# Forget gates by softplus with their scans moved forward, and the adaLN rows of the first FFN respread, in a two-layer diffusion trunk

## The chip, the cores and the metric

The kernel runs on one core of one Trainium2 chip. The metric is the device time of one execution in microseconds (us), taken as the median of several runs of the same program. Beside it stands one profiled execution, whose trace gives every time in this text that is shorter than the whole: PE is the matmul engine (TensorE), DVE is VectorE, ACT is ScalarE, POOL is GpSimd, SP is the engine from whose queue all weight transfers are issued.

## The reference

The trunk has two layers over 256 latent tokens and 256 context tokens of width 1024. A layer modulates its input (adaLN), runs four branches over it (a bidirectional mLSTM, differential attention, a 2-D Fourier mix, a spatial gating unit), merges them with sigmoid gates and a projection, and then runs a gated convolutional FFN. Two pieces matter here.

The modulation of a layer is a product of a conditioning vector with a large matrix; the six parts of 1024 are the shifts, scales and gates of the layer:

```python
mod  = (silu(c)     @ w_ada[l] + b_ada[l]).reshape(B, 6, 1, D)
modc = (silu(c_ctx) @ w_ada[l] + b_ada[l]).reshape(6, 1, D)
h = rmsnorm(x, norm_g[l, 0]) * (1.0 + mod[:, 1]) + mod[:, 0]
...
x = x + mod[:, 5] * rmsnorm(conv_ffn(h, ...), norm_g[l, 3])
```

The mLSTM takes per head, direction and token an input gate `ic` and a forget gate `fc`, the latter as a log sigmoid. Its decay weights come from running sums and running maxima over the tokens:

```python
fc = log_sigmoid(gg[:, 1])               # = -softplus(-gg)
b = cumsum(fc)
m_t = maximum(b + m, max over s of (b_t - b_s + ic_s))
wt = exp(b_t - b_s + ic_s - m_t)
```

## The kernel before, in words

All large products run on PE with each fp32 operand split into two fp32r parts, `hi` and `lo`, and three matmuls per product (`mm3`, L134 to L137). A weight tile is loaded by SP into a buffer `raw` (four of them), ACT writes `hi` from it (L122), and DVE or POOL writes `lo = raw - hi` (L131). PSUM results of these products use three buffers, so PE can't start a tile until the tile three before it has been read.

The program is written in one order; a scheduler with its own cost estimates then fixes the order of each engine's queue, by priority (the order of writing, shifted by `later(n)`) and by when it believes an instruction can start. At run time each engine takes its queue strictly in that order, SP's queue of transfers too. `issue_after(ins)` queues instructions on the engine of `ins` behind it.

**Gates.** In `mlstm()` the 16 gate columns `Gt` are turned by PE into `pg` (L983) and ACT adds the bias, `G` = mlG (L986). Input gates lie on partitions 0 to 3 (forward) and 32 to 35 (backward), forget gates on 64 to 67 and 96 to 99. L990 to L993 form the log sigmoid: DVE takes -|g| (mlE), ACT applies Exp and then Ln, DVE subtracts that from min(g, 0) (mlL). L1012 and L1013 copy the two groups of four rows down to partitions 0 and 32. Then come four scans of 256 tokens for the running sum `Bt` = mlB (L1007, two directions by two halves), `U = Bt - G` (L1016), four scans for the running minimum `NM` = mlNM (L1007), `EM = exp(NM - Bt)` = mlEM (L1019, L1020). PE turns U and EM into `pu` (L1027). The projections of q and k (`qk_tiles`: PE tiles qk, ACT L941 and L950, DVE L945, L947 and L951) are written after the gates but their matmuls run meanwhile; after `pu` PE goes on with the projection of the output gates (tile mm). `Bt` and `NM` are first set to zero by POOL (L928, L929). The tiles of this stage can be opened only when those of the spatial gating unit before it are done with.

**adaLN rows.** 128 outputs of the modulation are one row: a 512 KB transfer into a buffer `ar` and one product with a sum along the row on DVE (L232, `scalar_tensor_tensor` with an accumulator) for each conditioning vector. A row for latent and context tokens takes two such instructions (a junk and an ar one), a row for latent tokens alone one. `tick(n)` takes the next n rows of the list `todo`. 24 rows run in the mixer of layer 0 (one for each merged tile). In the FFN of layer 0, 56 rows run: 8 of layer 0 (part 5, the last gate), then 16 of layer 1 (its first shift and scale), all 24 with two instructions, then 32 of layer 1 with one. Three rows are taken after each up tile from the sixth on (`tu=3`), one after each down tile of the first two segments (`to=1`). The rows use two `ar` buffers, and the transfer of a row is written right before its product.

**FFN.** An up tile is 24 matmuls into `ua` and 24 into `ug` (512 columns in layer 0); ACT and DVE then form the convolution (ACT L1482, DVE L1486 and L1488), ACT the Silu (L1490), DVE the product with ug (L1491). 22 up tiles come in segments of 6, 8 and 8, each followed by the down products of the segment. Layer 1 begins with the modulation by rows 0 to 15 of its list (DVE L300).

Of the kernel before, what the change touches and what calls it, by code (L numbers as in the profile page):

```python
# [22 lines left out]
KF = 22  # L23
EPS = 1e-6
SEGS = ((0, 6), (6, 14), (14, 22))
CFG = dict(hi=4, raw=4, tb=0.6, tw=0.8, tw1=1.0, x1=2, mm=3, paddk=8, tk=4, acc=2, f3=(2, 2), qa=(0, 0), f0=(1, 1), f1=(1, 2), f2=(1, 2), n0=(1, 1), n1=(1, 1), hd=1, hq=3, na=48, tu=3, to=1, ka=2, yp=3, ph=400, kh=4, kt=4, ld=2, dl=2, W=2, h0=3, mix=1, keep=4, hot=400, nst=6, nb=1, pt=(1, 0), w1=14, w2=6, wd=(24,), ahead={7: (0, -1, 1), 0: (2,), 1: (3,)}, so=("mddddfddd", "mdpf", "mpf", "mrpfd0q"), xr="pppppppp", fw=(0, 2), g0="nddddddd", g1=("nddddddn", "nddddddn"), g3=("nddddddn", "ndndndnd"), gy="nddddddn", cm=1, h1=2, xp=2, pf=(1, 1), ck=1, ys=(1, 1, 1, 1), c0=1, te=0.8)
# [9 lines left out]
def trunk_kernel(ctx: ExitStack, tc: tile.TileContext, I, out):  # L36
    nc = tc.nc
# [39 lines left out]

    turn = [0.0, CFG["tb"]]
    todo = []
    sq = []  # L80
    hold = [None, False]
    wn = [0]
# [1 line left out]
    more_on = []  # L84
    x = {}

    def open_ada(stack, side, ns):
        pool = stack.enter_context(tc.tile_pool(name="adap", bufs=1, side=side))
        scb = pool.tile([128, ns, 1024], F32, name="scb")
        junk = pool.tile([128, 1024], mybir.dt.bfloat16, name="junk") if ns == 2 else None  # L90
        return pool, scb, junk

    def init_ada(ad):
        pool, scb, junk = ad
        ns = scb.shape[1]
        nc.sync.dma_start(out=scb, in_=I["ccb"][:, 0:ns, :])
        e = pool.tile([128, 1024], F32, name="ar", tag="ar", bufs=2)
# [56 lines left out]
    @contextmanager  # L154
    def later(n):
        p = tc.cur_priority
        tc.cur_priority = p + n
        yield
        tc.cur_priority = p + (tc.cur_priority - p - n)
# [64 lines left out]
            op=ALU.add)  # L224
        return ins_of(at)

    def ada_row(ad, i, m, ns, mod, vec):
        pool, scb, junk = ad
        raw = pool.tile([128, 1024], F32, tag="ar", name="ar", bufs=2)
        nc.sync.dma_start(out=raw, in_=I["w_adaT"][i])  # L230
        for st in range(ns):
            nc.vector.scalar_tensor_tensor(out=raw if st == ns - 1 else junk, in0=raw, scalar=0.5, in1=scb[:, st, :],  # L232
                                           op0=ALU.mult, op1=ALU.mult, accum_out=mod[:, m, st:st + 1])
        if m % 8 == 7:
            o = mod[:, m - 7:m + 1, 0:ns]
            nc.vector.tensor_tensor(
                out=o, in0=o, op=ALU.add,
                in1=vec[:, V_BA + m - 7:V_BA + m + 1].rearrange("p (a o) -> p a o", o=1).to_broadcast([128, 8, ns]))

    def mod_scale(vec, mod, chunk, gi, plus, ns=2, k0=0, k1=8, o=None):  # L240
        if o is None:
# [406 lines left out]
    def layer(l):  # L648
# [15 lines left out]
        with ExitStack() as es:  # L664
# [251 lines left out]
            def mlstm():  # L916
# [67 lines left out]
                U = w3.tile([128, T], F32, name="mlU", tag="mlU")  # L984
                G = wk.tile([128, 512], F32, tag="sq", name="mlG")
                nc.scalar.activation(out=G, in_=ps, func=AF.Identity, bias=vec[:, V_GB:V_GB + 1], scale=1.0)  # L986
                E1 = wk.tile([128, 512], F32, tag="t1", name="mlE")
                L1 = wk.tile([128, 512], F32, tag="t2", name="mlL")
                r = slice(64, 128)
                nc.vector.scalar_tensor_tensor(out=E1[r], in0=G[r], scalar=-1.0, in1=G[r], op0=ALU.mult, op1=ALU.min)  # L990
                nc.scalar.activation(out=E1[r], in_=E1[r], func=AF.Exp)
                nc.scalar.activation(out=E1[r], in_=E1[r], func=AF.Ln, bias=1.0, scale=1.0)
                nc.vector.scalar_tensor_tensor(out=L1[r], in0=G[r], scalar=0.0, in1=E1[r], op0=ALU.min, op1=ALU.subtract)  # L993

                def scans(dst, src, po, pi, d0, op0, op1, init):
                    for d in range(2):
                        o = slice(po[d], po[d] + 4)
                        i = slice(pi[d], pi[d] + 4)
                        if d == 0:
                            rng = (slice(256, 512), slice(0, 256))  # L1000
                            tail = 511
                        else:
                            rng = (slice(511, 255, -1), slice(255, None, -1))
                            tail = 256
                        for q in range(2):
                            a = d0[i].to_broadcast([4, 256]) if d0 is not None else src[i, rng[q]]
                            nc.vector.tensor_tensor_scan(out=dst[o, rng[q]], data0=a, data1=src[i, rng[q]],  # L1007
                                                         initial=init if q == 0 else dst[o, tail:tail + 1],
                                                         op0=op0, op1=op1)
# [285 lines left out]
            def sgu(early):  # L1295
# [16 lines left out]
                nc.sync.dma_start(out=sgw, in_=I["sgw"][l])  # L1312
                nc.sync.dma_start(out=sgb, in_=I["sgb"][l])
                sums = tiny.tile([128, 8], F32, tag="sums", name="sums")

                def take_sv(t2, ps):
                    for t in range(2):
                        with hot():
                            nc.scalar.activation(out=gv[:, t2 + t, :], in_=ps[:, t, :], func=AF.Gelu_apprx_tanh,
                                                 accum_out=sums[:, t2 + t:t2 + t + 1])  # L1320
# [48 lines left out]
            if not last or CFG["na"] < 40:  # L1369
                ad = open_ada(es, "left", ns)  # L1370
                init_ada(ad)
                todo.extend((lambda m=m: ada_row(ad, i0 + m, m, ns, mod, vec))
                            for m in range(CFG["na"] if last else 16, 40))
            diff(*(diff_tiles() if last else dqk))
            es3.close()
            fill(64)
# [87 lines left out]
        with ExitStack() as es:  # L1464
# [239 lines left out]
```

## Time and profile before

| | |
|---|---|
| median of 3 runs | 1406.83 us (1405.43 to 1408.57) |
| the profiled execution | 1407.98 us, of which the span of the engines' work is 1406.2 us |
| PE busy | 1336.9 us, 95% of the span |
| DVE busy | 863.8 us, 61% |
| POOL busy | 849.7 us, 60% |
| ACT busy | 621.6 us, 44% |
| mean granted PE clock | 0.983 of full speed |

A row of a timeline shows the start, the duration, the engine, the line, the instruction with its tiles (out<-in), how many were merged, and in brackets how long the engine had been idle before it and what ended that. A row of a list of waits shows who waited for whom: the time in total, how often, and the longest.

### The profile page before, as it was taken

Reading aid. Unit: us, or ns where it says so; the run is one execution under the profiler, and the core shown is the slowest. Engines: PE = TensorE matmul, PEld = TensorE weight load, DVE = VectorE, ACT = ScalarE, POOL = GpSimd, SP = SyncE. Lnnn points to the kernel's source line nnn. Section 1 sums busy time; section 2 is a strip of 40 time slices with the busy share of each in tenths; the row PEclk is TensorE's granted clock in tenths of the full one; section 3 lists DMA queues with packets and bytes.
Section 4 is the critical chain, followed back from the end, with each engine's and each line's share of the span. In section 5 each row is a group of like instructions: output and inputs, shape, how many; then the busy total and the mean of one; then the engine's idle time right before and its main releaser. Section 6 shows DMA issues by size and latency. Waiting matters only on the chain. (4 is left out here: it accounts for less than half of the span.)

```text
span 1406.2 us, 22765 instructions
## 1 busy us (share of the span) xinstructions
PE 1336.9 (95%) x8514; PEld 1195.1 (85%) x8514; DVE 863.8 (61%) x1554; ACT 621.6 (44%) x1098; POOL 849.7 (60%) x978
## 2 busy tenths in 40 slices
PE   8798999999999979999799999898999999899998
PEld 6597899888878979888688889897999998899997
DVE  4738766888777465599886553768847543532323
ACT  4435534444324445423231333466636545554443
POOL 1533234456764676567565546675556898689894
PEclk9999999999999999999899999999999999999999
DMA  9422223433443443466577443343324455355552
GB/s 347 137 77 81 69 105 106 135 120 140 160 162 107 147 151 114 138 227 211 195 253 270 155 160 106 116 135 104 108 76 135 147 164 184 123 184 200 183 181 75
DMA packets 61935, 210.55 MB, mean 150 GB/s; under 512 B 7145, under 2 KB 9729, under 8 KB 61569
## 3 DMA queue, kind: packets, MB, share of 16 engines
q1 hardware_dynamic: 61824, 209.10, 44.1%
q8 instruction: 67, 1.10, 0.3%
q14 instruction: 44, 0.35, 0.1%
HBM read 208.01 MB, written 1.06 MB: 149 GB/s over the span
## 5 line engine op out<-in xcount | busy, mean ns | idle before, releaser
L131 POOL TENSOR_TENSOR lo<-raw,hi 128x256 fp32r<-128x256 f32 x814 | 698.6, 890 | 392.2 <-ACT hi L122 373.9
L122 ACT CAST hi<-raw 128x1024 fp32r<-128x1024 f32 (+2 forms) x284 | 293.7, 1036 | 336.1 <-PE ua L136 76.6
L131 DVE TENSOR_TENSOR lo<-raw,hi 128x1024 fp32r<-128x1024 f32 (+2 forms) x79 | 122.3, 1548 | 89.6 <-ACT hi L122 89.5
L135 PE MATMUL gt<-hh,hi 128*128 128x512 f32 (+1 forms) x512 | 175.3, 342 | 1.0 <-DVE sig L782 1.0
L137 PE MATMUL gt<-hh,lo 128*128 128x512 f32 (+1 forms) x512 | 172.8, 338 | 0.6 <-POOL lo L131 0.6
L136 PE MATMUL gt<-hl,hi 128*128 128x512 f32 (+1 forms) x512 | 172.2, 336 | 0.0
L135 PE MATMUL ug<-hh,hi 128*128 128x256 f32 (+1 forms) x384 | 125.9, 328 | 10.4 <-DVE ca L1488 10.4
L232 DVE SCALAR_TENSOR_TENSOR ar<-ar,scb 128x1024 f32<-128x1024 f32 x80 | 122.4, 1534 | 15.6 <-DMA ar<-w_adaT 14.8
L136 PE MATMUL ug<-hl,hi 128*128 128x256 f32 (+1 forms) x384 | 125.5, 327 | 0.0
L135 PE MATMUL ua<-hh,hi 128*128 128x256 f32 (+1 forms) x384 | 124.3, 324 | 0.9 <-ACT hh L301 0.9
L137 PE MATMUL ug<-hh,lo 128*128 128x256 f32 (+1 forms) x384 | 125.1, 326 | 0.0
L136 PE MATMUL ua<-hl,hi 128*128 128x256 f32 (+1 forms) x384 | 124.0, 323 | 0.1
L137 PE MATMUL ua<-hh,lo 128*128 128x256 f32 (+1 forms) x384 | 123.8, 322 | 0.0
L137 PEld LDWEIGHTS gt<-hh,lo 128*128 128x128 f32 x512 | 96.6, 189 | 11.6 <-POOL lo L131 0.8
L135 PEld LDWEIGHTS gt<-hh,hi 128*128 128x128 f32 x512 | 96.7, 189 | 11.0 <-DVE sig L782 1.2
L136 PEld LDWEIGHTS gt<-hl,hi 128*128 128x128 f32 x512 | 96.8, 189 | 10.0
L135 PEld LDWEIGHTS ug<-hh,hi 128*128 128x128 f32 x384 | 74.2, 193 | 16.9 <-issue 8.5
L135 PE MATMUL o<-fh,hi 128*128 128x256 f32 (+1 forms) x240 | 81.0, 337 | 0.0
L136 PE MATMUL mm<-lo,hh 128*128 128x256 f32 x272 | 78.6, 289 | 2.4 <-DVE lo L131 2.4
L136 PE MATMUL o<-fl,hi 128*128 128x256 f32 (+1 forms) x240 | 80.5, 335 | 0.0
L137 PE MATMUL o<-fh,lo 128*128 128x256 f32 (+1 forms) x240 | 80.5, 335 | 0.0
L135 PEld LDWEIGHTS ua<-hh,hi 128*128 128x128 f32 x384 | 72.8, 190 | 7.6 <-ACT hh L301 1.1
(312 smaller groups left out, 3250.6 us busy)
## 6 DMA issues: line engine op xcount, KB each, us to landing
raw<-w_up SPq DMA_DIRECT2D x92, 512.0 KB, 4.0
ar<-w_adaT SPq DMA_DIRECT2D x80, 512.0 KB, 4.1
raw<-w_gate SPq DMA_DIRECT2D x64, 512.0 KB, 3.5
raw<-w_tm SPq DMA_DIRECT2D x24, 512.0 KB, 3.5
raw<-w_dr SPq DMA_DIRECT2D x22, 512.0 KB, 3.5
raw<-w_dn SPq DMA_DIRECT2D x20, 512.0 KB, 3.7
ada_w<-w_ada SPq DMA_DIRECT2D x16, 512.0 KB, 8.3
raw<-w_branch SPq DMA_DIRECT2D x16, 512.0 KB, 3.6
```

What stands on the lines that cost most here:

```text
L122: nc.scalar.copy(hi[:, :n], raw[:, :n])
L131: e.tensor_tensor(out=lo[:, s], in0=raw[:, s], in1=hi[:, s].bitcast(F32), op=ALU.subtract)
L135: nc.tensor.matmul(ps, a[0], b[0], start=start, stop=False)
L136: nc.tensor.matmul(ps, a[0], b[1], start=False, stop=False)
L137: return nc.tensor.matmul(ps, a[1], b[0], start=False, stop=stop)
L232: nc.vector.scalar_tensor_tensor(out=raw if st == ns - 1 else junk, in0=raw, scalar=0.5, in1=scb[:, st, :], op0=ALU.mult, op1=ALU.mult, ac ...
```

## The change

The log sigmoid is written as -softplus(-g): one ACT instruction with the Softplus table reads the forget gates on partitions 64 to 99 and writes partitions 0 to 35, and the sum is scanned with a subtraction. The backward scans run over 512 tokens in one instruction. The sums, U and the minima get a priority 200 places earlier. The Softplus table is asked for right after the last Gelu of the spatial gating unit. The adaLN rows of both places load one row ahead (the transfer of the next row is written before the product of this one); in the FFN of layer 0 they get three buffers, the 24 rows with two instructions are mixed evenly among the 32 with one, and up tiles take two and three rows in turn.

```diff
-CFG = dict(..., tu=3, ...)
+CFG = dict(..., tu=2.5, ..., gs=200)
...
+    due = [0.0]
-    def open_ada(stack, side, ns):
+    def open_ada(stack, side, ns, bufs=2):
...
     def tick(n=1, after=None):
         for _ in range(n):
             if todo:
-                if after is None:
-                    todo.pop(0)()
-                else:
-                    with tc.issue_after(after):
-                        todo.pop(0)()
+                row = todo.pop(0)
+                row.load()
+                for ahead in todo[:row.bufs // 2]:
+                    ahead.load()
+                with tc.issue_after(after) if after is not None else ExitStack():
+                    row.run()
...
-    def ada_row(ad, i, m, ns, mod, vec):
-        pool, scb, junk = ad
-        raw = pool.tile([128, 1024], F32, tag="ar", name="ar", bufs=2)
-        nc.sync.dma_start(out=raw, in_=I["w_adaT"][i])
...
+    class AdaRow:
...
+        def load(self):
+            if self.raw is None:
+                self.raw = self.pool.tile([128, 1024], F32, tag="ar", name="ar", bufs=self.bufs)
+                nc.sync.dma_start(out=self.raw, in_=I["w_adaT"][self.i])
+
+        def run(self):      # the products and the bias as before
...
-                E1 = wk.tile([128, 512], F32, tag="t1", name="mlE")
-                L1 = wk.tile([128, 512], F32, tag="t2", name="mlL")
-                r = slice(64, 128)
-                nc.vector.scalar_tensor_tensor(out=E1[r], in0=G[r], scalar=-1.0, in1=G[r], op0=ALU.mult, op1=ALU.min)
-                nc.scalar.activation(out=E1[r], in_=E1[r], func=AF.Exp)
-                nc.scalar.activation(out=E1[r], in_=E1[r], func=AF.Ln, bias=1.0, scale=1.0)
-                nc.vector.scalar_tensor_tensor(out=L1[r], in0=G[r], scalar=0.0, in1=E1[r], op0=ALU.min, op1=ALU.subtract)
...
-                        if d == 0:
-                            rng = (slice(256, 512), slice(0, 256))
-                            tail = 511
-                        else:
-                            rng = (slice(511, 255, -1), slice(255, None, -1))
-                            tail = 256
-                        for q in range(2):
+                        rng = (slice(256, 512), slice(0, 256)) if d == 0 else (slice(511, None, -1),)
+                        for q in range(2 - d):
...
-                nc.vector.tensor_copy(L2[0:4], L1[64:68])
-                nc.vector.tensor_copy(L2[32:36], L1[96:100])
-                scans(Bt, L2, (0, 32), (0, 32), onec, ALU.mult, ALU.add, 0.0)
+                nc.scalar.activation(out=L2[0:36], in_=G[64:100], func=AF.Softplus, scale=-1.0)
                 q = slice(0, 36)
-                nc.vector.tensor_tensor(out=U[q], in0=Bt[q], in1=G[q], op=ALU.subtract)
-                scans(NM, U, (0, 32), (0, 32), None, ALU.min, ALU.min, 0.0)
+                with later(-CFG["gs"]):
+                    scans(Bt, L2, (0, 32), (0, 32), onec, ALU.mult, ALU.subtract, 0.0)
+                    nc.vector.tensor_tensor(out=U[q], in0=Bt[q], in1=G[q], op=ALU.subtract)
+                    scans(NM, U, (0, 32), (0, 32), None, ALU.min, ALU.min, 0.0)
...
                 tm_proj(5, NTQ, take_sv)
+                table(AF.Softplus, gelu[0])
...
-                ad = open_ada(es, "left", ns)
-                todo.extend((lambda m=m: ada_row(ad, i0 + m, m, ns, mod, vec)) for m in range(40, 48))
+                ad = open_ada(es, "left", ns, 3)
+                todo.extend(AdaRow(ad, i0 + m, m, ns, mod, vec) for m in range(40, 48))
             if l == 0:
-                todo.extend((lambda m=m: ada_row(ad, 32 + m, m, 2 if m < 16 else 1, mods[1], P[1]["vec"]))
-                            for m in range(CFG["na"]))
+                nxt = [AdaRow(ad, 32 + m, m, 2 if m < 16 else 1, mods[1], P[1]["vec"]) for m in range(CFG["na"])]
+                two, lone = todo + nxt[:16], nxt[16:]
+                todo.clear()
+                for j, row in enumerate(lone):
+                    while two and len(two) * len(lone) > (len(lone) - j - 1) * 24:
+                        todo.append(two.pop(0))
+                    todo.append(row)
...
                     if i > CFG["tk"]:
-                        tick(1 if last else CFG["tu"], at[0])
+                        due[0] += 1 if last else CFG["tu"]
+                        n = int(due[0])
+                        due[0] -= n
+                        tick(n, at[0])
```

## Rows read from the trace of the kernel before

**Rows 1.** The waits of PE over the whole span: total, times, longest.
```profile
PE ug L135 <- DVE ca L1488: 10.4, 3, 7.7
```
**Rows 2.** Timeline of PE, gates of layer 1.
```profile
967.56 0.43 PE L1027 MATMUL pu<-cst,mlU 36*128 36x36 f32 x4
974.68 0.64 PE L1027 MATMUL pu<-cst,mlEM 36*128 36x36 f32 x4 [6.69 <-ACT mlEM L1020]
```
**Rows 3.** Timeline of PE, gates of layer 0.
```profile
123.61 0.44 PE L1027 MATMUL pu<-cst,mlEM 36*128 36x36 f32 x4 [1.45 <-ACT mlEM L1020]
...
128.18 0.39 PE L136 MATMUL mm<-lo,hh 128*128 128x256 f32 x1 [2.39 <-DVE lo L131]
```
**Rows 4.** Stretches after these waits: length, busy time by engine, granted PE clock, DMA share, GB/s.
```profile
128.00:134.00 6.00, 5.82 (x36) 5.82 (x37) 5.15 (x8) 1.95 (x3) 1.86 (x2) 0.72 0.48 170
975.00:980.00 5.00, 5.00 (x28) 4.93 (x28) 4.88 (x11) 3.69 (x6) 0.00 (x0) 0.58 0.17 69
680.00:689.00 9.00, 8.30 (x26) 6.72 (x27) 8.17 (x12) 3.28 (x5) 1.55 (x1) 0.69 0.53 180
```
**Rows 5.** Timeline of DVE, FFN of layer 0.
```profile
676.86 1.22 DVE L232 SCALAR_TENSOR_TENSOR junk<-ar,scb 128x1024 bf16<-128x1024 f32 x1 [3.86 <-DMA ar<-w_adaT]
...
679.81 0.74 DVE L1488 SCALAR_TENSOR_TENSOR ca<-ua,vec,ca 128x510 f32<-128x510 f32 x1
...
681.31 0.69 DVE L1491 TENSOR_TENSOR ca<-ca,ug 128x512 f32<-128x512 f32 x1 [0.76 <-ACT ca L1490]
```
**Rows 6.** DVE by line, 600 to 700 us: count, busy, mean ns, idle before.
```profile
L232 DVE SCALAR_TENSOR_TENSOR ar<-ar,scb 128x1024 f32<-128x1024 f32 x23 | 35.1, 1528 | 0.4
L232 DVE SCALAR_TENSOR_TENSOR junk<-ar,scb 128x1024 bf16<-128x1024 f32 x22 | 30.2, 1374 | 7.8 <-DMA ar<-w_adaT 7.8
L131 DVE TENSOR_TENSOR lo<-raw,hi 128x1024 fp32r<-128x1024 f32 (+1 forms) x7 | 12.0, 1712 | 0.0
```
**Rows 7.** Timeline of PE: the first ua and ug of two neighbouring up tiles.
```profile
688.58 0.39 PE L135 MATMUL ua<-hh,hi 128*128 128x512 f32 x1
...
699.46 0.39 PE L135 MATMUL ua<-hh,hi 128*128 128x512 f32 x1
```
**Rows 8.** The waits of SP's queue, 590 to 830 us.
```profile
SPq L230 <- DVE ar L232: 101.6, 45, 6.2
```
**Rows 9.** Timeline of DVE: the last adaLN row, and the first modulation of layer 1.
```profile
821.33 1.22 DVE L232 SCALAR_TENSOR_TENSOR ar<-ar,scb 128x1024 f32<-128x1024 f32 x1
...
901.95 0.87 DVE L300 SCALAR_TENSOR_TENSOR t<-x,ms,R 128x256 f32<-128x256 f32 x2 [3.96 <-POOL lo L131]
```
**Rows 10.** Timeline of ACT, gates of layer 1.
```profile
950.32 0.69 ACT L986 ACTIVATE mlG<-pg,vec 128x512 f32<-128x512 f32 x1
...
955.99 1.28 ACT L991 ACT_TABLE_LOAD   x1 [1.59 <-DVE mlE L990]
...
974.00 0.62 ACT L1020 ACTIVATE mlEM<-mlEM 36x512 f32<-36x512 f32 x1
```
**Rows 11.** Timeline of DVE, gates of layer 1.
```profile
962.61 1.39 DVE L1007 TENSOR_TENSOR_SCAN mlB<-one,mlL 4x256 f32<-4x256 f32 x2
...
968.09 2.38 DVE L1007 TENSOR_TENSOR_SCAN mlNM<-mlU 4x256 f32<-4x256 f32 x2
...
973.29 0.67 DVE L1019 TENSOR_TENSOR mlEM<-mlNM,mlB 36x512 f32<-36x512 f32 x1
```
**Rows 12.** Timeline of POOL, layer 1.
```profile
956.03 0.52 POOL L928 MEMSET mlB<- 128x512 f32 x1
...
965.15 3.62 POOL L131 TENSOR_TENSOR lo<-raw,hi 128x256 fp32r<-128x256 f32 x4 [5.35 <-ACT hi L122]
969.20 3.91 POOL L131 TENSOR_TENSOR lo<-raw,hi 128x256 fp32r<-128x256 f32 x4 [0.43 <-ACT hi L122]
```
**Rows 13.** Timeline of DVE, layer 0.
```profile
113.42 2.19 DVE L1007 TENSOR_TENSOR_SCAN mlB<-one,mlL 4x256 f32<-4x256 f32 x2
...
126.39 1.74 DVE L131 TENSOR_TENSOR lo<-raw,hi 128x1024 fp32r<-128x1024 f32 x1
```

More of the change, by code (lines that the diff above doesn't have):

```diff
@@ L25 @@
 SEGS = ((0, 6), (6, 14), (14, 22))
-CFG = dict(hi=4, raw=4, tb=0.6, tw=0.8, tw1=1.0, x1=2, mm=3, paddk=8, tk=4, acc=2, f3=(2, 2), qa=(0, 0), f0=(1, 1), f1=(1, 2), f2=(1, 2), n0=(1, 1), n1=(1, 1), hd=1, hq=3, na=48, tu=3, to=1, ka=2, yp=3, ph=400, kh=4, kt=4, ld=2, dl=2, W=2, h0=3, mix=1, keep=4, hot=400, nst=6, nb=1, pt=(1, 0), w1=14, w2=6, wd=(24,), ahead={7: (0, -1, 1), 0: (2,), 1: (3,)}, so=("mddddfddd", "mdpf", "mpf", "mrpfd0q"), xr="pppppppp", fw=(0, 2), g0="nddddddd", g1=("nddddddn", "nddddddn"), g3=("nddddddn", "ndndndnd"), gy="nddddddn", cm=1, h1=2, xp=2, pf=(1, 1), ck=1, ys=(1, 1, 1, 1), c0=1, te=0.8)
+CFG = dict(hi=4, raw=4, tb=0.6, tw=0.8, tw1=1.0, x1=2, mm=3, paddk=8, tk=4, acc=2, f3=(2, 2), qa=(0, 0), f0=(1, 1), f1=(1, 2), f2=(1, 2), n0=(1, 1), n1=(1, 1), hd=1, hq=3, na=48, tu=2.5, to=1, ka=2, yp=3, ph=400, kh=4, kt=4, ld=2, dl=2, W=2, h0=3, mix=1, keep=4, hot=400, nst=6, nb=1, pt=(1, 0), w1=14, w2=6, wd=(24,), ahead={7: (0, -1, 1), 0: (2,), 1: (3,)}, so=("mddddfddd", "mdpf", "mpf", "mrpfd0q"), xr="pppppppp", fw=(0, 2), g0="nddddddd", g1=("nddddddn", "nddddddn"), g3=("nddddddn", "ndndndnd"), gy="nddddddn", cm=1, h1=2, xp=2, pf=(1, 1), ck=1, ys=(1, 1, 1, 1), c0=1, te=0.8, gs=200)
 C_ID, C_MF, C_MB, C_RC, C_RS, C_SEL, C_ONE, C_END = 0, 128, 256, 384, 448, 512, 514, 515
@@ L90, in open_ada @@
         junk = pool.tile([128, 1024], mybir.dt.bfloat16, name="junk") if ns == 2 else None
-        return pool, scb, junk
+        return pool, scb, junk, bufs
     def init_ada(ad):
-        pool, scb, junk = ad
+        pool, scb, junk, bufs = ad
         ns = scb.shape[1]
         nc.sync.dma_start(out=scb, in_=I["ccb"][:, 0:ns, :])
-        e = pool.tile([128, 1024], F32, name="ar", tag="ar", bufs=2)
+        e = pool.tile([128, 1024], F32, name="ar", tag="ar", bufs=bufs)
         for st in range(ns):
@@ L225, in ada_fin, with __init__ @@
         return ins_of(at)
-    def ada_row(ad, i, m, ns, mod, vec):
-        pool, scb, junk = ad
-        raw = pool.tile([128, 1024], F32, tag="ar", name="ar", bufs=2)
-        nc.sync.dma_start(out=raw, in_=I["w_adaT"][i])
[L231 to L238, printed above, removed]
+    class AdaRow:
+        def __init__(self, ad, i, m, ns, mod, vec):
+            self.pool, self.scb, self.junk, self.bufs = ad
+            self.i, self.m, self.ns, self.mod, self.vec, self.raw = i, m, ns, mod, vec, None
+        def load(self):
[3 more added lines that the diff above has]
+        def run(self):
+            m, ns, mod, raw = self.m, self.ns, self.mod, self.raw
+            for st in range(ns):
+                nc.vector.scalar_tensor_tensor(out=raw if st == ns - 1 else self.junk, in0=raw, scalar=0.5,
+                                               in1=self.scb[:, st, :], op0=ALU.mult, op1=ALU.mult,
+                                               accum_out=mod[:, m, st:st + 1])
+            if m % 8 == 7:
+                o = mod[:, m - 7:m + 1, 0:ns]
+                b = self.vec[:, V_BA + m - 7:V_BA + m + 1].rearrange("p (a o) -> p a o", o=1).to_broadcast([128, 8, ns])
+                nc.vector.tensor_tensor(out=o, in0=o, op=ALU.add, in1=b)
     def mod_scale(vec, mod, chunk, gi, plus, ns=2, k0=0, k1=8, o=None):
@@ L998, in scans @@
                         i = slice(pi[d], pi[d] + 4)
-                        if d == 0:
-                            rng = (slice(256, 512), slice(0, 256))
-                            tail = 511
-                        else:
-                            rng = (slice(511, 255, -1), slice(255, None, -1))
-                            tail = 256
-                        for q in range(2):
-                            a = d0[i].to_broadcast([4, 256]) if d0 is not None else src[i, rng[q]]
+                        rng = (slice(256, 512), slice(0, 256)) if d == 0 else (slice(511, None, -1),)
+                        for q in range(2 - d):
+                            a = d0[i].to_broadcast([4, 256 * (d + 1)]) if d0 is not None else src[i, rng[q]]
                             nc.vector.tensor_tensor_scan(out=dst[o, rng[q]], data0=a, data1=src[i, rng[q]],
-                                                         initial=init if q == 0 else dst[o, tail:tail + 1],
+                                                         initial=init if q == 0 else dst[o, 511:512],
                                                          op0=op0, op1=op1)
                 L2 = wk.tile([128, 512], F32, tag="acc", name="mlL2", bufs=CFG["acc"])
-                nc.vector.tensor_copy(L2[0:4], L1[64:68])
-                nc.vector.tensor_copy(L2[32:36], L1[96:100])
-                scans(Bt, L2, (0, 32), (0, 32), onec, ALU.mult, ALU.add, 0.0)
+                nc.scalar.activation(out=L2[0:36], in_=G[64:100], func=AF.Softplus, scale=-1.0)
                 q = slice(0, 36)
-                nc.vector.tensor_tensor(out=U[q], in0=Bt[q], in1=G[q], op=ALU.subtract)
-                scans(NM, U, (0, 32), (0, 32), None, ALU.min, ALU.min, 0.0)
+                with later(-CFG["gs"]):
+                    scans(Bt, L2, (0, 32), (0, 32), onec, ALU.mult, ALU.subtract, 0.0)
+                    nc.vector.tensor_tensor(out=U[q], in0=Bt[q], in1=G[q], op=ALU.subtract)
+                    scans(NM, U, (0, 32), (0, 32), None, ALU.min, ALU.min, 0.0)
                 EM = wk.tile([128, 512], F32, tag="t1", name="mlEM")
@@ L1314, in sgu @@
                 sums = tiny.tile([128, 8], F32, tag="sums", name="sums")
+                gelu = [None]
                 def take_sv(t2, ps):
@@ L1318, in take_sv @@
                         with hot():
-                            nc.scalar.activation(out=gv[:, t2 + t, :], in_=ps[:, t, :], func=AF.Gelu_apprx_tanh,
-                                                 accum_out=sums[:, t2 + t:t2 + t + 1])
+                            gelu[0] = ins_of(nc.scalar.activation(
+                                out=gv[:, t2 + t, :], in_=ps[:, t, :], func=AF.Gelu_apprx_tanh,
+                                accum_out=sums[:, t2 + t:t2 + t + 1]))
                 tm_proj(5, NTQ, take_sv)
+                table(AF.Softplus, gelu[0])
                 mean = tiny.tile([128, 4], F32, tag="mean", name="mean")
@@ L1371, in layer @@
                 init_ada(ad)
-                todo.extend((lambda m=m: ada_row(ad, i0 + m, m, ns, mod, vec))
-                            for m in range(CFG["na"] if last else 16, 40))
+                todo.extend(AdaRow(ad, i0 + m, m, ns, mod, vec) for m in range(CFG["na"] if last else 16, 40))
             diff(*(diff_tiles() if last else dqk))
```

## The prediction

> **What bounds the kernel now.** I read the list of waits by engine first, then the timelines around PE's longest ones, then DVE's work by line in those places. PE is busy 1336.9 of 1406.2 us, so the kernel is bound by PE and only PE's idle time (69.3 us) and its clock can be won. The longest line in the list of PE's waits is a wait of the ug matmuls for the convolution on DVE [rows 1]. 7.7 us of its 10.4 are one stop, which DVE's timeline puts at 673 to 680.6 us, when that convolution ends [rows 5]. The gates hold three more: PE waits 6.69 us for EM in layer 1 [rows 2], and in layer 0 1.45 us for EM and 2.39 us for a lo [rows 3]. The change touches these four places, 18.2 us; PE's other waits lie at the start of the program, in the norms between the stages, and in the merges, where nothing is edited.
>
> Each of the three stops is followed by a stretch at the lower of PE's two clock levels, 1.2 instead of 2.4 GHz. The length of the stretch times what is missing from the granted clock is the time lost: 0.28 of 6 us is 1.7 us, 0.42 of 5 us is 2.1 us, 0.31 of 9 us is 2.8 us [rows 4], of which some 0.35 us fell in the wait itself, leaving 2.4. If PE does not stop, this comes back too. The most that can be won is then 7.7 + 2.4 = 10.1 us in the FFN, 6.7 + 2.1 = 8.8 us in layer 1, 3.8 + 1.7 = 5.5 us in layer 0: 24.4 us.
>
> **The adaLN rows.** DVE is full where the rows with two products lie: 45 products took 65.3 us of the 100 us before 700, 1.45 us each [rows 6]. At 680 two things met: DVE had a backlog, and the product at the head of its queue waited 3.86 us for its transfer, with the convolution behind it [rows 5]. PE, with three PSUM buffers, waited for that convolution.
>
> An up tile takes PE 10.88 us [rows 7]. On DVE it costs 0.74 + 0.74 + 0.69 = 2.2 us for ca [rows 5], the first convolution taken as long as the second, and lo: two weight tiles, 0.4 of them on DVE (the counter adds 0.6 per tile and POOL takes it at 1), so 0.8 x 1.71 = 1.4 us [rows 6]. Three rows with two products are 6 x 1.45 = 8.7 us: 12.3 us together, over the 10.88. Mixed, the 56 rows hold 80 products, 1.43 a row, so 2.5 rows are 3.6 products or 5.2 us: 8.8 us together. The fullest up tile of the new order has five products, 7.3 us, so 10.9 us: just full, and it comes once in the first pair and once at the end of the second segment, between emptier ones. The load does not vanish, it moves: the lone rows at the end had three products per up tile and get 3.6.
>
> The list now lasts longer. Rows taken: 5 in the two up tiles of the first segment, 8 in its down products, 20, 8, and 15 left, which are done at the sixth up tile of the last segment; before it was 6 + 8 + 24 + 8 and 10 left, done at the fourth. The last row moves from 821 us [rows 9] by two up tiles to some 843, less what is won. Row 53 of the list (counted from 0) is the last that layer 1 needs at its first modulation, at 902 us [rows 9]: 59 us of cover. The 8 rows of the last gate of layer 0 are at places 0 to 16, taken before the end of the fourth up tile's share of the second segment, and are needed only after the last segment's up tiles.
>
> The transfers: 80 in all, as before, each 512 KB. What changes is SP's queue. SP waited 101.6 us in 45 of the 56 loads of this stretch for a buffer `ar` [rows 8], with weight loads queued behind. With two buffers the load of row j waits for the product of row j-2; with three, written one row ahead, the load of row j+1 waits for that same product. So at the moment when row j was asked for before, row j+1 is asked for now, a whole row sooner, and DVE is no longer behind, so the wait itself shortens. A row is one or two products and their pause, 4.4 us if 2.5 of them share an up tile, against a worst delay of 3.86 us [rows 5]. I take 9.6 of the 10.1 us. If the cover failed once more at another place, it would cost again what it costs now, about 10 us. In the mixer of layer 0 the rows come one per merged tile and PE waits for none of them: nothing.
>
> **The gates, layer 1.** G is done at 951.0 us [rows 10]. Before, scans could only start at 962.6 [rows 11] because two DVE instructions, Exp, Ln and two table loads stood between. Softplus is not in this trace; its nearest row is the Exp of EM over the same 36 x 512, 0.62 us [rows 10], and at most it is Exp, Ln and their loads again, 2 x (0.62 + 1.28) = 3.8 us. Its own table load (1.28 us by the same row) stands before G, when ACT is waiting for the value projection. By either value its result is there at 951.6 to 954.8, and the scans then wait for something else: POOL zeroes Bt at 956.03, so they start at 956.6 [rows 12]. A scan over 256 tokens takes 0.70 us at best and 1.19 at worst [rows 11]. One over 512 lies between one and two of them, 0.7 and 1.4 (2.4 slow); I take 1.4, since nothing in the rows says that the second half is cheaper. Bt is then 2 x 0.7 + 1.4 = 2.8 us, U 0.67 (taken as long as the subtraction for EM of the same shape [rows 11]), NM 2.8, EM 0.67, a table load 1.28 and Exp 0.62: 956.6 + 8.8 = 965.4. With scans at 1.19, and U and EM taken as slow, it is 956.6 + 4.8 + 1.2 + 4.8 + 1.2 + 1.9 = 970.5. PE comes to `pu` at 967.56 [rows 2], so EM is 2.2 us early or 2.9 us late; before, 6.7 late. What is late next is DVE's queue: from 962.6 on its scans and the queue behind them run to 973 and beyond [rows 11], and the convolutions of q and k must read PSUM before PE's next tile mm can start. The edit takes mlE, mlL and two copies off that queue, some 2.7 us if each is taken at the 0.67 of the subtraction for EM [rows 11]. I expect about 1.6 us to stay of the 8.8 and take 7.2.
>
> The Trainium skill bears on the slow value: SBUF — State Buffer, section Who interferes with whom, says that a DVE instruction with two SBUF inputs contends with a GpSimd instruction that reads SBUF, and that the second to start blocks fully. The rows agree in kind: the sums at 962.6 took 0.70 us each while POOL stood idle, the minima at 968 1.19 us while it was making lo [rows 11, 12]. POOL's lo also surrounds the place to which the scans move, so by that rule the late end, 970.5, would be the one to expect. It is priced as the second case below.
>
> **The gates, layer 0.** The same chain had its scans at 113.42 [rows 13]; by layer 1's rows G precedes the scans there by 12 us [rows 10, 11]. Moved up by 6 us, as in layer 1, EM is ready well before PE's `pu` at 122.2, by both values of a scan. The 2.39 us wait is a lo that DVE began at 126.39 [rows 13], behind the scans and convolutions; it has to come 3.9 us sooner to be hidden (2.39 + 1.45). The same 2.7 us of DVE work disappear and the scans fill idle time that DVE spent waiting for Exp and Ln. I take 4.8 of 5.5.
>
> **Sum.** 9.6 + 7.2 + 4.8 = 21.6 us. The profiled execution took 1407.98, so 1386.4; it lies 1.15 above the median of the runs, which gives 1385.2. New small waits somewhere in a schedule that is laid out anew: about 1 us. **1386 us.**
>
> **Rivals.**
> - *Layer 1 keeps its wait.* DVE's queue, not the gate chain, is the limit there, the scans run at their slow rows, and PE stops for 3 us plus its stretch at the low clock: 5 of the 8.8 stay. 1386 + 3.5 = 1389.5. For it: the scans at 1.19 us in [rows 11]. Against: the work taken off.
> - *The FFN stop moves.* Rows run on through two more up tiles and the fullest has five products; a late transfer meets a full DVE once more. 1386 + 9.6 = 1395.6.
> - *Nothing comes of it.* PE arrives earlier at waits whose end does not move (the norms between layers, weights not yet split by POOL, which is 60% busy over the span), and these take it back: 1406, within 0.2% of before. Against it: where PE was not stopped, two neighbouring up tiles follow at the bare sum of their matmuls [rows 7], so weights were there ahead of it.
> - *Slower.* SP issues in order. If the loads written ahead hold SP waiting for an `ar` buffer while the next up tile's weights stand behind them, each of the 16 up tiles from the sixth to the last but one starts late. The point from which it decides is 22 / 16 = 1.4 us per up tile; at 2 us per tile it is 1386 + 32 = 1418. For it: SP already waits 101.6 us there [rows 8]. Against: three buffers for two, and products that run on time.
>
> **Chances.** The forecast 0.58, layer 1 keeps its wait 0.20, the FFN stop moves 0.09, nothing 0.06, slower 0.07. A difference under 0.2% (2.8 us) can't be told from none here. The first three cases are faster: 0.87; same 0.06; slower 0.07. The likeliest case alone spans 1382.5 (all 24.4 won, 1406.83 - 24.4) to 1390. The range for 8 in 10 reaches up to the moved FFN stop: 1382 to 1397.
>
> **What would show it.** In the new profile: no wait of ug for ca over 1 us between 590 and 850; DVE with gaps in every up tile there, where 600 to 700 had next to none; the junk products' waits for `ar` well under the 7.8 us of [rows 6]; no Exp or Ln load in the gates, Softplus once per layer right behind G, scans of Bt at about 957 in layer 1 and 107 in layer 0; waits of `pu` for EM under 2 us; the granted clock 1.00 in the stretches of [rows 4]. The prediction is wrong if PE still stops at `pu`, if a new wait of PE for DVE or SP of more than 5 us appears, or if a table load of Tanh falls between the early Softplus load and its use.

## The result, and the profile after

The changed kernel takes 1392.18 us (median of 4 runs, 1390.05 to 1396.08) against 1406.69 us before (4 runs): ratio 0.9899, 95% interval 0.9874 to 0.9924, 14.5 us faster. The forecast was 1386, the range 1382 to 1397. The profiled execution of the changed kernel is its longest run, 1396.08 us with a span of 1394.3, so the two traces differ by 11.9 us of span. The same kernel profiled once more (change_again below) has a span of 1391.9, 14.3 less than before.

PE's waits in the list of the whole span: the 7.7 us stop of ug for ca is gone, and what is left on that line is mainly a wait of 2.4 us at 522 us, ahead of the edited rows, that was there before too (2.42 us); `pu` no longer appears; and two lines have grown, qk (0.3 before) and gt for sig (one wait of 1.0 before).

```profile
PE qk L137 <- DVE qk L957: 3.2, 1, 3.2
PE ug L137 <- DVE ca L1488: 2.7, 2, 2.4
PE gt L137 <- DVE sig L792: 2.2, 2, 1.2
```

The stretches of [rows 4] in the new kernel, and first the one with and behind its new wait in layer 1 (the granted clock is the number behind the last bracket):

```profile
950.00:960.00 10.00, 6.83 (x24) 5.32 (x23) 7.23 (x13) 6.59 (x12) 1.38 (x3) 0.83 0.15 54
128.00:134.00 6.00, 6.00 (x52) 6.00 (x51) 4.85 (x8) 2.46 (x5) 5.10 (x6) 1.00 0.29 91
680.00:689.00 9.00, 9.00 (x42) 7.44 (x41) 8.21 (x12) 2.97 (x5) 6.98 (x6) 1.00 0.85 288
```

**Where the time went.** Six instructions of PE that stand in every version cut the span into stretches. In the new trace they are:

```profile
65.15 0.67 PE L877 MATMUL f<-PQ,dft 128*128 128x258 f32 x2 [0.63 <-DVE PQ L871]
334.60 0.47 PE L1235 MATMUL ds<-st,st 128*128 128x512 f32 x1 [0.69 <-DVE st L1217]
879.11 0.58 PE L172 MATMUL st<-one,sq 128*128 128x1 f32 x4 [0.74 <-DVE sq L295]
906.26 1.08 PE L857 MATMUL f<-dft,ft 128*128 128x256 f32 x2 [2.01 <-ACT ft L832]
1013.39 0.66 PE L735 MATMUL pt<-cst,fsq 128*128 128x128 f32 x4 [0.95 <-DVE fsq L728]
1194.53 0.79 PE L503 MATMUL hT<-dg,xa 128*128 128x128 f32 x2 [4.85 <-DVE dg L497]
```

The differences of their starts, in each profiled execution (us; the names are those of the experiments below):

| | to f | f to ds: layer 0's gates | ds to st: its FFN | st to ft: norms | ft to pt: layer 1's gates | pt to hT: its merge | hT to end |
|---|---|---|---|---|---|---|---|
| before | 64.3 | 275.2 | 553.7 | 26.0 | 108.5 | 179.7 | 198.9 |
| the change | 65.2 | 269.5 | 544.5 | 27.2 | 107.1 | 181.1 | 199.8 |
| change_again | 65.1 | 269.4 | 545.1 | 25.9 | 105.6 | 181.2 | 199.7 |
| gates_only | 66.0 | 269.4 | 555.5 | 26.8 | 105.9 | 181.2 | 200.1 |
| rows_only | 64.7 | 275.3 | 545.0 | 26.4 | 108.7 | 179.7 | 199.3 |
| rows_ahead | 65.3 | 275.2 | 550.1 | 26.3 | 108.6 | 179.6 | 199.2 |
| rows_mix | 64.2 | 275.8 | 548.1 | 25.4 | 110.4 | 179.7 | 199.3 |
| rows_25 | 64.1 | 273.7 | 554.5 | 26.7 | 108.8 | 179.8 | 199.3 |
| old_log | 64.6 | 273.0 | 545.2 | 26.3 | 105.2 | 181.1 | 198.6 |
| conv_first | 64.8 | 269.5 | 544.5 | 26.0 | 102.6 | 181.3 | 199.7 |
| conv_first_2 | 64.0 | 270.0 | 544.8 | 26.0 | 102.6 | 179.7 | 198.8 |
| conv_sm | 65.3 | 270.1 | 544.9 | 25.4 | 104.2 | 180.6 | 198.6 |
| no_prefetch | 65.6 | 269.5 | 544.9 | 26.2 | 108.8 | 181.1 | 200.0 |
| scan4 | 64.9 | 270.1 | 545.2 | 26.4 | 106.3 | 179.7 | 198.7 |

Layer 0's gates give 5.7 us and the FFN 9.2, both close to the forecast. Layer 1's gates give only 1.3 (2.9 in change_again), and its merge takes 1.4 back. The profiled execution loses some 1.6 us of layer 1's stretch before the gates begin: G starts 32.7 us after ft, against 31.2 before and in change_again, and the granted clock from 905 to 912 us is 0.76, against 1.00 in change_again.

**The FFN.** DVE's groups between 600 and 700 us, against [rows 6], and SP's wait for a buffer, against [rows 8]: there are 35 products instead of 45, and the junk products wait 2.4 us for a transfer instead of 7.8. The third line, from DVE's list of waits over the same 100 us, shows that DVE is no longer behind: its product with ug now waits for PE.

```profile
L242 DVE SCALAR_TENSOR_TENSOR ar<-ar,scb 128x1024 f32<-128x1024 f32 x25 | 37.8, 1538 | 0.0
L242 DVE SCALAR_TENSOR_TENSOR junk<-ar,scb 128x1024 bf16<-128x1024 f32 x10 | 16.0, 1598 | 2.4 <-DMA ar<-w_adaT 2.4
DVE ca L1491 <- PE ug L139: 8.4, 4, 2.4
```

```profile
SPq L237 <- DVE ar L242: 78.6, 39, 6.3
```

**Layer 0's gates**, against [rows 3, 13]: the scans start at 106.82, and `pu` follows without a wait, as does the tile behind it.

```profile
106.82 2.30 DVE L1005 TENSOR_TENSOR_SCAN mlB<-one,mlL 4x256 f32<-4x256 f32 x2 [0.51 <-POOL mlB L938]
```

```profile
122.80 0.41 PE L1025 MATMUL pu<-cst,mlEM 36*128 36x36 f32 x4
```

**Layer 1's gates**, against [rows 2, 10, 11]. DVE's timeline, then PE's, then ACT's. The first row of the sums, and the first of the minima, merges a scan over 256 tokens with the one over 512 (0.68 and 1.58 us, 0.82 and 1.22 us):

```profile
945.25 2.29 DVE L1005 TENSOR_TENSOR_SCAN mlB<-one,mlL 4x256 f32<-4x256 f32 x2 [1.82 <-POOL mlB L938]
947.58 1.05 DVE L1005 TENSOR_TENSOR_SCAN mlB<-one,mlB,mlL 4x256 f32<-4x256 f32 x1
948.73 0.97 DVE L1014 TENSOR_TENSOR mlU<-mlB,mlG 36x512 f32<-36x512 f32 x1
949.63 0.47 DVE L955 SCALAR_TENSOR_TENSOR qk<-qk,vec,qk 128x255 f32<-128x255 f32 x1
950.03 2.06 DVE L1005 TENSOR_TENSOR_SCAN mlNM<-mlU 4x256 f32<-4x256 f32 x2
952.12 0.74 DVE L1005 TENSOR_TENSOR_SCAN mlNM<-mlU,mlNM 4x256 f32<-4x256 f32 x1
952.79 0.45 DVE L957 SCALAR_TENSOR_TENSOR qk<-qk,vec,qk 128x255 f32<-128x255 f32 x1
```

```profile
953.38 0.47 PE L137 MATMUL qk<-hh,hi 128*128 128x512 f32 x1 [3.17 <-DVE qk L957]
...
960.91 0.41 PE L1025 MATMUL pu<-cst,mlEM 36*128 36x36 f32 x4
```

```profile
939.71 0.63 ACT L1010 ACTIVATE mlL<-mlG 36x512 f32<-36x512 f32 x1
...
942.97 0.56 ACT L951 ACTIVATE qk<-qk,vec 128x256 f32<-128x256 f32 x1
...
953.31 1.28 ACT L960 ACT_TABLE_LOAD   x1 [9.79 <-DVE qk L957]
...
954.93 0.61 ACT L1018 ACTIVATE mlEM<-mlEM 36x512 f32<-36x512 f32 x1
```

EM is ready at 955.5, and PE comes to `pu` at 960.6 without a wait for it. Most of these 5.1 us are PE's own delay, though. The first q/k tile was ready for its convolution at 943.5 (L951 ends), while DVE stood idle for POOL's memset. The two convolution steps (L955, L957) are queued between and behind the scans, until 953.2. They read that tile's PSUM buffer, one of three, and PE's fourth q/k tile needs it: 3.17 us of wait, and then 0.17 x 10 = 1.7 us lost at the lower clock. In the kernel before, DVE's timeline has the same two steps ahead of the scans, in the time in which DVE waited for Exp and Ln:

```profile
958.53 0.48 DVE L945 SCALAR_TENSOR_TENSOR qk<-qk,vec,qk 128x255 f32<-128x255 f32 x1 [2.63 <-ACT qk L941]
...
961.20 0.48 DVE L947 SCALAR_TENSOR_TENSOR qk<-qk,vec,qk 128x255 f32<-128x255 f32 x1
```

Measured from ft, which leaves the earlier gains out, PE came to `pu` 48.4 us after it before the change and EM was ready at 55.5; in change_again EM is ready at 47.7 and PE comes at 52.8.

### The profile page after: what moved, and what is told of

It is laid out like the page before. It is cut to its first block, busy times and chain, and to the rows that moved or that the text cites. A ratio compares the mean times of both kernels' runs of the same rounds, so it can differ in the third digit from the quotient of the medians.

```text
span 1394.3 us, 22736 instructions
## 1 busy us (share of the span) xinstructions
PE 1339.0 (96%) x8514; PEld 1196.5 (86%) x8514; DVE 856.8 (61%) x1542; ACT 618.5 (44%) x1096; POOL 852.5 (61%) x978
## 5 line engine op out<-in xcount | busy, mean ns | idle before, releaser
L133 DVE TENSOR_TENSOR lo<-raw,hi 128x1024 fp32r<-128x1024 f32 (+2 forms) x79 | 114.2, 1446 | 87.0 <-ACT hi L124 87.0
L138 PEld LDWEIGHTS ua<-hl,hi 128*128 128x128 f32 x384 | 73.1, 190 | 6.8 <-DVE hl L312 0.5
```

Source lines behind the costliest of these rows:

```text
L133: e.tensor_tensor(out=lo[:, s], in0=raw[:, s], in1=hi[:, s].bitcast(F32), op=ALU.subtract)
L138: nc.tensor.matmul(ps, a[0], b[1], start=False, stop=False)
```

## The experiments

Each ratio is to the kernel before, run beside it on the same chip; in brackets stands its 95% interval.

**The halves.** gates_only makes only the edits in `mlstm()` and the Softplus table request; rows_only makes only those to `tick`, `AdaRow`, the order of the list and `tu`; change_again is the change itself.

> The gate edits alone (softplus, early scans, its table prefetch); the adaLN rows as before. By the reading of the two traces layer 0 gives 5.7 us and layer 1 only 2.9, because PE's fourth q/k tile waits some 3.2 us for the first tile's convolution behind the scans: 1406.7 - 8.6 = 1398.1 us, with that wait of qk for DVE in layer 1 and the FFN stop of 7.7 us for ca still there. By the prediction's own terms it would be 4.8 + 7.2 = 12.0: 1394.7 us, and no such wait. If the qk wait comes from the rows' new order and not from the scans, it is absent here and layer 1 gives up to 8.8: 1392.2 us.

> The adaLN edits alone; the gates as before. By the reading of the traces the FFN stop is worth 9.1 us and the 2.7 us lost between the layers is a chance of the clock: 1406.7 - 9.1 = 1397.6 us, and the waits of PE for EM in both layers stay (1.5 and 6.7 us). If the longer list of rows is what costs the 2.7 us between the layers, it is 1406.7 - 6.4 = 1400.3 us, with the granted clock of that stretch at 0.80 again. If the FFN stop moves: 1406.

> The changed kernel once more. If the 2.7 us lost between the layers (granted clock 0.80 at 875 to 900 us) are a chance of one execution, that stretch has the clock of the kernel before (about 0.95) here or is again different, with a span of 1389 to 1392 us; if the change causes them, the clock is 0.80 there again. The 3.17 us wait of qk for DVE and 1.18 us wait of gt for sig belong to the order of instructions and must show again.

Measured: gates_only 0.9951 (0.9934 to 0.9968), rows_only 0.9940 (0.9921 to 0.9959), change_again 0.9884 (0.9864 to 0.9903), median 1392.93. The halves add up: 0.49% + 0.60% = 1.09% against 1.16%. They are 6.9 and 8.5 us, nearest to the first value of each expectation (8.6 and 9.1). PE's timeline of gates_only has the FFN stop and, without any new row order, the wait of qk:

```profile
677.06 0.77 PE L135 MATMUL ug<-hh,hi 128*128 128x512 f32 x1 [8.13 <-DVE ca L1479]
...
963.17 0.47 PE L135 MATMUL qk<-hh,hi 128*128 128x512 f32 x1 [3.18 <-DVE qk L947]
```

So that wait comes from the gate edits. In rows_only it is absent and `pu` waits its 6.69 us again. The 2.7 us between the layers, of which the expectations speak, are the 1.2 us of the norms stretch (26.0 to 27.2) and the 1.6 us before G. change_again, the same kernel, has neither: they belong to one execution, and the theory that the longer list costs there falls. The 1.5 us of layer 1's merge are there in gates_only and not in rows_only; more below.

**The first convolution ahead of the scans.** In layer 1 the first q/k tile is written before the scans, and the scans are queued behind its second convolution step (`conv[0]`):

```diff
...
+                if last:
+                    qk_tiles(0, 1)
-                with later(-CFG["gs"]):
+                with later(-CFG["gs"]), after(conv[0]):
...
-                qk_tiles(CFG["qa"][l], 4)
+                qk_tiles(int(last), 4)
```

> The whole change, and in layer 1 the scans are issued after the convolution of the first q/k tile, which only needs DVE's idle time before the memset of mlB. If that convolution's place in DVE's queue causes the 3.17 us wait of the fourth q/k tile and the low clock behind it (1.75 us), both go: 1392.2 - 4.9 = 1387.3 us, and EM (ready at about 955 in the run of the change) still comes in time for pu, which PE then reaches at about 955.7. If EM is late instead, PE stops at pu for up to 3 us: 1390.5 us. If the wait is for something else on DVE (the scans' own length), it only moves: 1392 us.

> conv_first once more, beside conv_sm. If the stretch of layer 1's gates (ft to the pt of fsq, 102.6 us) belongs to the order, it shows within 0.5 us again, and the time is 2 to 3 us under the change.

Measured: 1390.13 (1389.00 to 1391.14), ratio 0.9865 (0.9843 to 0.9887), against change_again's 1392.03 to 1393.67 on the same chip; and the second time 1388.08 (1387.53 to 1389.92), 0.9857 (0.9839 to 0.9875). It is faster than the kernel before and, by 2.8 us in the median, than the change. DVE's timeline and the stretch of the wait:

```profile
941.03 0.48 DVE L957 SCALAR_TENSOR_TENSOR qk<-qk,vec,qk 128x255 f32<-128x255 f32 x1
942.21 2.29 DVE L1006 TENSOR_TENSOR_SCAN mlB<-one,mlL 4x256 f32<-4x256 f32 x2 [0.70 <-POOL mlB L938]
```

```profile
950.00:960.00 10.00, 9.75 (x74) 8.93 (x73) 9.70 (x17) 6.65 (x10) 7.03 (x8) 1.00 0.32 97
```

The convolution fits into the idle time before the memset, the scans start 37.4 us after ft as in change_again, the wait of qk is gone, and the clock is 1.00. The place of the convolution in DVE's queue is thereby shown as the cause. It gave 3.0 us of the 4.9 (105.6 to 102.6): PE, earlier now, meets waits of 0.66 us for the tile tho, 0.43 and 0.22 for W and 0.25 for a convolution. EM is now ready 47.0 us after ft and PE comes to `pu` at 47.8, so the chain of the gates has 0.8 us to spare.

**The parts of the adaLN edit,** each alone on the kernel before. rows_ahead: three buffers and the load ahead (`tu=3`, old order). rows_mix: mixed order and `tu=2.5` (two buffers, no load ahead). rows_25: `tu=2.5` alone.

> Of the adaLN edits only the third buffer and the load one row ahead; 3 rows per up tile in the old order, gates as before. If the late transfer made the FFN stop, the load ahead takes all of it: some 9 us under the kernel before (ratio 0.9936), and no wait of ug for ca over 1 us after 590 us. If DVE's load made it (12.3 us of work for an up tile of 10.88), the wait for the transfer goes but DVE stays behind: a stop of some 4 us or several smaller ones remain, 4 to 5 us won (0.997).

> Of the adaLN edits only the mixed order and 2.5 rows per up tile; two buffers, each row loaded when its turn comes, gates as before. If DVE's load made the stop, all of it goes: some 9 us (0.9936), although DVE goes on waiting for ar. If the late transfer made it, DVE still waits up to 3.9 us for ar with the convolution behind it, and PE for ca; with more room on DVE between, a wait of 1 to 4 us stays: 4 to 8 us won (0.994 to 0.997).

> Of the adaLN edits only 2.5 rows per up tile; old order (rows with two products first), two buffers, no load ahead, gates as before. Five products per up tile are 7.3 us, with ca and lo 10.9 of 10.88: DVE just full. If load alone counts, the backlog no longer grows and the stop goes: some 9 us (0.9936). If mixing or the earlier load is needed, a wait for a transfer can't be caught up with no room left: a stop of some 4 us stays, 4 to 5 us won (0.997).

Measured: rows_ahead 0.9995 (0.9986 to 1.0004), rows_mix 0.9968 (0.9958 to 0.9979), rows_25 1.0016 (1.0006 to 1.0027). PE's timelines, of rows_ahead, of rows_25 and of rows_mix:

```profile
676.64 0.57 PE L137 MATMUL ug<-hh,hi 128*128 128x512 f32 x1 [2.08 <-DVE ca L1497]
...
691.31 0.47 PE L137 MATMUL ug<-hh,hi 128*128 128x512 f32 x1 [1.95 <-DVE ca L1497]
```

```profile
677.53 0.77 PE L137 MATMUL ug<-hh,hi 128*128 128x512 f32 x1 [6.21 <-DVE ca L1497]
...
703.50 0.47 PE L137 MATMUL ug<-hh,hi 128*128 128x512 f32 x1 [1.48 <-DVE ca L1497]
```

```profile
846.32 0.36 PE L137 MATMUL o<-fh,hi 128*128 128x256 f32 x1 [0.51 <-DVE mod L248]
...
851.30 0.39 PE L138 MATMUL o<-fl,hi 128*128 128x256 f32 x1 [2.15 <-POOL fl L1502]
```

Load ahead removes 7.7 - 4.0 = 3.7 us of the wait itself and leaves DVE behind, as the theory of the load had it; its gain in the runs is smaller still than expected, 0.7 us, and where the rest of the 3.6 us that its profiled execution wins in the FFN goes in the median is open. Fewer rows a tile alone leave the whole 7.7 us (6.21 + 1.48) and made it 2.2 us slower. There DVE's timeline shows the late transfer at work, with the convolution behind it, longer than the 3.86 us of [rows 5]:

```profile
673.68 1.23 DVE L242 SCALAR_TENSOR_TENSOR junk<-ar,scb 128x1024 bf16<-128x1024 f32 x1 [5.89 <-DMA ar<-w_adaT]
```

Mixing, with the fewer rows, removes the stop of ug entirely, although DVE still waits 28.9 us for transfers between 590 and 850 (18.1 + 10.8, against 22.6 before), none of them longer than 2.7 us. But its last row's product starts only at 844.28 (839.44 in rows_only, where DVE's waits for transfers are 7.0 us), and PE waits at the end of the last segment, at 846 and 851, with the clock at 0.89 from 846 to 862. In the runs the parts alone give 0.7 us (load ahead), 4.5 (mixed order with fewer rows) and -2.2 (fewer rows); all three together, rows_only, give 8.5. Either cause is enough for a stop: the load with no late transfer (rows_ahead), a late transfer with less load (rows_25). So the load has to be spread, and with the earlier transfers the spread list ends sooner. Both theories were half right. The mixed order without the fewer rows, and the third buffer without the load ahead, no run shows.

**The parts of the gate edit.** old_log keeps all else and forms the log sigmoid with Exp and Ln as before, without the request for the Softplus table; no_prefetch drops `table(AF.Softplus, gelu[0])`; scan4 cuts the backward scans into two of 256 again.

> The whole change, but the forget gates by the old way (Exp and Ln with their two loads, two DVE steps, two copies); the scans in their new form, the adaLN rows as changed. If the softplus is what brings the gates forward, the waits of PE for EM are back in both layers (1.5 and 4 to 7 us): the rows' 9 us and at most 2 more are won (0.992 to 0.9935). If the form of the scans and DVE's order were enough, the gates keep their gain: 14 us or more (0.990 or less).

> The whole change without the early table load for Softplus: the load then stands between G and Softplus in both layers. In the run of the change Softplus ended at 940.3 and the scans started at 945.3, after POOL's memset of mlB; 1.28 us more fit into that gap, so the time is that of the change within 0.1%. If the load pushes the q/k and split work on ACT behind it instead, PE waits about 1.3 us more per layer: up to 2.6 us slower than the change (ratio 0.990).

> The whole change with the scan against time in two pieces of 256 again in place of one of 512. In the run of the change one of 512 took 1.58 and 1.22 us, pieces of 256 0.68 to 1.05. If two pieces cost what one long one costs, nothing moves: the time of the change, within 0.1%. If a piece has a start-up of its own of some 0.3 us, the convolution behind the scans and PE's wait of qk come 0.6 us later: not to be told from the change either in the runs, but to be read from the wait (3.8 in place of 3.2 us).

Measured: old_log 0.9919 (0.9906 to 0.9933), no_prefetch 0.9891 (0.9873 to 0.9909), scan4 0.9888 (0.9871 to 0.9906). PE's timeline of old_log:

```profile
123.16 0.43 PE L1033 MATMUL pu<-cst,mlEM 36*128 36x36 f32 x4 [0.72 <-ACT mlEM L1026]
...
127.73 0.39 PE L138 MATMUL mm<-lo,hh 128*128 128x256 f32 x1 [2.40 <-DVE lo L133]
...
961.77 0.43 PE L1033 MATMUL pu<-cst,mlEM 36*128 36x36 f32 x4 [3.86 <-ACT mlEM L1026]
```

The softplus is worth 273.0 - 269.4 = 3.6 us in layer 0. In layer 1 it is worth nothing as the change is laid out (105.2 against 105.6): a wait of 3.86 us for EM stands against one of 3.17 for qk. It does bring EM forward there, from 52.5 us after ft in old_log to 47.7 in change_again; the wait of qk takes this back. old_log thus gained 11.4 us, a little more than the 11 it was given at most: its two stretches with gates are 2.1 and 3.3 us shorter than before, without softplus. What does this, the longer scans or their place in DVE's queue, isn't shown. no_prefetch and scan4 can't be told from the change by the runs: their intervals hold its ratio, and that of no_prefetch also holds the 0.990 of its second theory. The profiled execution of no_prefetch is its slowest run, 5 us above its median. In it the scans again start right behind POOL's memset (943.23, after 3.21 us of idle time), though its queue is otherwise laid out anew and qk waits 4.33 us instead of 3.17. In scan4 qk waits 3.95, close to the 3.8 of the second theory there. What the priority of 200 places does by itself no run shows.

**The product in the merge.** The 1.5 us of layer 1's merge lie at one DVE instruction, the product of sm and neglam (128 x 1). conv_sm makes it a tensor_scalar on top of conv_first:

```diff
-nc.vector.tensor_tensor(out=sm[:, 1:2], in0=sm[:, 1:2], in1=neglam, op=ALU.mult)
+nc.vector.tensor_scalar(out=sm[:, 1:2], in0=sm[:, 1:2], scalar1=neglam, scalar2=None, op0=ALU.mult)
```

> As conv_first, and the product of sm and neglam (128 x 1) in the last branch of the mixer is a tensor_scalar with neglam as the scalar, not a tensor_tensor. In the runs with the new gates this product took 2.57 us once in layer 1 (0.16 alone), until POOL's run of eight lo had ended, and PE then waited 1.19 us for sig behind it; the stretch from the pt of fsq to hT takes 1.5 us more than before. If a DVE instruction of two tensors from SBUF is what POOL holds up, the product takes under 0.7 us, that wait goes and the stretch is back near 179.7: 1.5 us under conv_first. If the one-tensor form is held up alike (E scaled by sm took 1.04 us beside POOL, 0.47 alone), it stays at about 181.2 and the time is that of conv_first.

Measured: 1390.14 (1387.00 to 1390.79), 0.9863 (0.9846 to 0.9881): not faster than conv_first_2 beside it. The product took 0.21 us, but the wait did not go and the stretch is 180.6, so the expectation came out on neither side. First conv_first, then conv_first_2, the same kernel, POOL's and DVE's timelines:

```profile
1088.87 5.63 POOL L133 TENSOR_TENSOR lo<-raw,hi 128x256 fp32r<-128x256 f32 x8
```

```profile
1091.94 2.58 DVE L1249 TENSOR_TENSOR sm<-sm,neglam 128x1 f32<-128x1 f32 x1
```

```profile
1088.71 6.27 POOL L133 TENSOR_TENSOR lo<-raw,hi 128x256 fp32r<-128x256 f32 x8
```

```profile
1091.79 0.46 DVE L1249 TENSOR_TENSOR sm<-sm,neglam 128x1 f32<-128x1 f32 x1
```

And conv_sm, DVE's timeline (POOL's run of eight lo lasts there from 1091.37 to 1096.98):

```profile
1094.38 0.21 DVE L1249 TENSOR_SCALAR sm<-sm,neglam 128x1 f32<-128x1 f32 x1
1094.52 2.75 DVE L1250 TENSOR_SCALAR E<-E,sm 128x512 f32<-128x512 f32 x1
```

In conv_first the product ends at 1094.52, when POOL's run ends (1094.50). In conv_first_2, with the same order and the same offset of 3.1 us, it goes through at once and POOL's run is longer instead. With the form changed the hold-up moved to the next instruction, and PE still waits 1.09 us for sig. The single execution decides, then, though not alone: of the eight profiled executions with new gates and the old form six show it (all but conv_first_2 and scan4), of the five with old gates none. What sets the odds stays open.

## Why the prediction was right, and where its sizes were off

The direction and the range held, and so did the mechanisms in the FFN and in layer 0. Of the cases it named, the one that came true is the first rival, "layer 1 keeps its wait" (1389.5, chance 0.20), and not the likeliest: 1392.2 lies above the 1390 up to which that one spans. That the range still holds it is in part luck, for its upper end was drawn for an FFN stop that moves, and the stop did not.

*FFN stop, 9.6 us:* 9.2 in the profiled execution, 8.5 to 9.2 in the others with both edits. The stop did not move, the clock there is 1.00, and the last row's product starts at 833.5 us, where 843 less the 9 us won was forecast. That neither load ahead nor fewer rows alone would do, the prediction did not say; it listed them as one.

*Gates of layer 0, 4.8 us:* 5.7 (5.1 to 5.8 in the other executions with both edits and softplus). Both waits and the low clock are gone, as the prediction's upper value of 5.5 had it. The scans start at 106.82, forecast 107.

*Gates of layer 1, 7.2 us:* the mis-sized term, 1.3 in the profiled execution and 2.6 to 2.9 in change_again and gates_only. The chain itself came later than the sum had it: from ft, EM was forecast for 46.3 us (965.4 less 919.15, the start of ft before the change) and is ready at 47.7 in change_again, 0.7 us and not 2.2 ahead of the 48.4 at which PE had come to `pu` before. The scans start at 37.4, as forecast. One over 512 tokens, taken at 1.4, took 1.58 and 1.22 us. What failed is the sentence on what is late next. It named DVE's queue and the convolutions that must read PSUM, but for the tile mm behind `pu`, with 1.6 us to stay. The wait came sooner, at the fourth q/k tile, whose buffer is freed by the first tile's convolution; the early scans (DVE's work from 945.25 to 952.9) stand between. It costs 3.2 + 1.7 us, and 0.8 more in new waits of the tile SC behind it; 8.8 - 5.7 = 3.1 is what remains, and change_again has 2.9.

The prediction set against this the late end of the chain, 51.4 us after ft (970.5), with all scans slow. In the trace scans did run slower beside POOL's lo: 1.58 us against 1.22 over 512 tokens, 1.05 against 0.74 over 256. That agrees in kind with the Trainium skill, SBUF — State Buffer, section Who interferes with whom, by which a DVE instruction with two SBUF inputs contends with a GpSimd instruction that reads SBUF. But only some of the scans met lo, none was blocked for a whole run of POOL, and the end came at 47.7, between the two values and nearer the early one.

*New small waits, 1 us:* too little. The merge took 1.4 by the hold-up on DVE; the start and the last FFN took 0.8 and 0.9 in the profiled execution, and conv_first_2 loses nothing there, so these belong to single executions.

## What to carry to other kernels

When a chain is moved forward on an engine, read the instructions it now stands in front of, and for each that frees a PSUM buffer count tiles to the matmul that needs it: here three buffers meant that the first tile's convolution was due before the fourth tile. Use the idle time ahead of the moved chain (here, DVE waiting for a memset) for that reader. An edit of several parts can be worth more than the sum of them, where one removes the load and the next the late transfer (here 8.5 us against 0.7 + 4.5): test parts together before dropping one.

## What the runs showed of the hardware

A DVE product of 128 x 1 took 0.16 us alone, 0.46 us in one execution beside POOL and 2.58 us in another of the same kernel, until POOL's eight back-to-back instructions had all ended; POOL's eight took 6.27 us where DVE came through and 5.63 where it did not. The Trainium skill, SBUF — State Buffer, section Who interferes with whom, has DVE and GpSimd lock each other out for an instruction, and says that tensor_scalar can contend as well; conv_sm agrees (2.75 us, 0.47 alone). That the hold lasted over more than three POOL instructions of 0.70 us, and fell on one execution and not on the other, only these runs show.

One Softplus over 36 x 512 took 0.63 us, as much as the Exp of [rows 10], and its table load 1.28 us.
